# Halves of an array swapped by DMA alone: whole rows on both queues in place of one half of the columns on each

## The chip, the cores and the metric

The kernel runs on one core of a Trainium2 chip. The metric is the device time of one execution in microseconds (us); lower is better. The core has compute engines, which do nothing here but a few start-up fills, and 16 DMA engines, which move the data. SP (SyncE) and ACT (ScalarE) each issue DMAs into a queue of their own, called q1 and q10 in the profile; both queues are served by the same 16 DMA engines.

## The reference

```
x = np.random.randn(8192, 8192).astype(np.float32)
return np.fft.ifftshift(x)
```

With even sizes this swaps the quadrants: `out[r, c] = x[(r + 4096) % 8192, (c + 4096) % 8192]`. There is no arithmetic. 268.44 MB are read from the device's main memory (HBM) and 268.44 MB are written to it. A row has 32 KB, half a row 16 KB; the right half of each source row becomes the left half of a row of the output, and the left half the right.

## The kernel before

Every DMA goes straight from `x` to `out`, both in HBM. `copy` (lines 28 to 33) issues one: it is given a queue, a first row and column of the output, and the dimensions as pairs of step and count, which hold for both sides; line 29 works out where the source begins. `rows` is 16 x 16 = 256, so the 8192 rows make 32 blocks of 256.

The loops of lines 43 to 48 go through the blocks from the last to the first, four at a time. For each block SP's queue moves the left half of the output rows (line 45: 256 pieces of 16 KB, 4 MB) and ACT's queue a right half (line 48), in the order 1, 0, 3, 2 within the four while SP goes 3, 2, 1, 0. A DMA of 256 rows has 16 neighbouring rows for each DMA engine. Thus SP reads only right halves of `x` and writes only left halves of `out`, and ACT the other way round.

One of ACT's DMAs, that of the block that begins at `start` (line 35), leaves out its last 16 rows (line 47) and has 240. Those 16 half rows are moved ahead of the loops in four strips of 1024 columns (4 KB). Three of the strips are cut into two DMAs, of 14 and 2, 9 and 7, and 4 and 12 rows, and the fourth has all 16 rows (lines 36 to 41): seven DMAs with 64 pieces in all.

The order in a queue is the order of the program. The framework gives the DMAs eight completion semaphores in turn, and an issue waits until the DMA that last used its semaphore has landed; so four of a queue's large DMAs are under way at a time. Nothing else is waited for until the end, where SP waits for the last of them (line 74).

Of the kernel before, what the change touches and what calls it, by code (L numbers as in the profile page):

```python
# [1 line left out]

# [4 lines left out]


ENGINES = 16


@with_exitstack
def kernel(
    ctx: ExitStack,
    tc: tile.TileContext,
    x: bass.AP,
    out: bass.AP,
):


    nc = tc.nc
    R, C = x.shape
    hr = R // 2
    hc = C // 2
    per = 16
    rows = ENGINES * per

    def copy(queue, row, col, dims):
        src = (row + hr) % R * C + (col + hc) % C
        queue.dma_start(  # L30
            out=bass.AP(out.tensor, out.offset + row * C + col, dims),
            in_=bass.AP(x.tensor, x.offset + src, dims),
        )

    start = R - 3 * rows
    strip = hc // 4
    for n, k in enumerate((14, 9, 4)):
        col = hc + n * strip
        copy(nc.scalar, start + rows - ENGINES, col, [[C, k], [1, strip]])
        copy(nc.scalar, start + rows - ENGINES + k, col, [[C, ENGINES - k], [1, strip]])  # L40
    copy(nc.scalar, start + rows - ENGINES, hc + 3 * strip, [[C, ENGINES], [1, strip]])

    for first in range(R - 4 * rows, -1, -4 * rows):
        for n in (3, 2, 1, 0):
            copy(nc.sync, first + n * rows, 0, [[C, rows], [1, hc]])
            right = first + (n + 2) % 4 * rows
            left_out = ENGINES if right == start else 0
            copy(nc.scalar, right, hc, [[C, rows - left_out], [1, hc]])


# [1 line left out]
_INS = ['x']  # L52
_OUTS = [((8192, 8192), 'float32')]


# [23 lines left out]
```

## Time and profile before

| | us |
|---|---|
| median of 3 runs | 822.09 (822.01 to 822.77) |
| profiled execution | 821.95 |
| its span, first to last instruction | 820.2 |
| SP's issues, first to last | 0.7 to 700.4 |
| ACT's issues, first to last | 0.7 to 726.2 |
| from issue to landing, a 4 MB DMA (median) | 101.7 (SP), 102.0 (ACT) |

The profile counts what the 16 DMA engines moved as packets; a packet here is one piece of a DMA on one engine, and a completion write of 4 bytes counts as a packet as well. "GB/s" is what was read, and as much was written in the same time. The span is shown in 40 slices of 20.5 us each. A DMA issue is short on the engine that issues it; its landing is the time at which all of its data and its completion have arrived. The line number of all issues is that of the helper, line 30.

### The profile page before, as it was taken

To read this page: it belongs to the slowest core of one execution; us is meant where nothing else is said; L and a number is where in the kernel's file an instruction comes from. 1 tells how busy PE (TensorE), PEld (TensorE's weight loads), DVE (VectorE), ACT (ScalarE), POOL (GpSimd) and SP (SyncE) were. 2 spreads that over 40 slices of the span, in tenths; PEclk is the share of its full clock that TensorE was granted. 3 is DMA by queue.
4 is the path that set the end of the run, shared out by engine and by line. 5 is a ranking of instruction groups with operands and counts; after the bars stand their busy time and mean duration, and the time that the engine had idled before them with its cause. 6 is when DMAs were issued, how large, how long until landed. Compare 5 with 4: busy or idle time off the path is not lost. (4 is left out here: it accounts for less than half of the span.)

```text
span 820.2 us, 116 instructions
## 1 busy us (share of the span) xinstructions
POOL 0.2 (0%) x4
## 2 busy tenths in 40 slices
POOL 0000000000000000000000000000000000000000
DMA  9999999999999999999999999999999999999998
GB/s 301 329 324 331 331 328 326 327 330 333 335 330 327 332 328 329 332 329 333 324 331 328 322 336 328 332 324 329 328 328 331 327 333 329 328 330 331 325 328 285
DMA packets 17520, 268.44 MB, mean 327 GB/s; under 512 B 1088, under 2 KB 1088, under 8 KB 1152
## 3 DMA queue, kind: packets, MB, share of 16 engines
q1 hardware_dynamic: 8704, 134.22, 51.3%
q10 hardware_dynamic: 8816, 134.22, 47.9%
HBM read 268.44 MB, written 268.44 MB: 655 GB/s over the span
## 5 line engine op out<-in xcount | busy, mean ns | idle before, releaser
L63 POOL MEMSET const-uint8-127<- 128x1 uint8 x1 | 0.1, 103 | 0.0
L63 POOL MEMSET const-bfloat16-1.0<- 128x1 bf16 x1 | 0.1, 102 | 0.0
L63 POOL MEMSET const-float32-0.0<- 128x1 f32 x1 | 0.1, 99 | 0.2 <-issue 0.2
L63 POOL MEMSET const-float32-1.0<- 128x1 f32 x1 | 0.1, 99 | 0.0
## 6 DMA issues: line engine op xcount, KB each, us to landing
out_dram<-in_x_dram SPq DMA_DIRECT2D x32, 4096.0 KB, 101.7
out_dram<-in_x_dram ACTq DMA_DIRECT2D x31, 4096.0 KB, 102.0
out_dram<-in_x_dram ACTq DMA_DIRECT2D x1, 3840.0 KB, 29.3
out_dram<-in_x_dram ACTq DMA_DIRECT2D x1, 64.0 KB
out_dram<-in_x_dram ACTq DMA_DIRECT2D x1, 56.0 KB
out_dram<-in_x_dram ACTq DMA_DIRECT2D x1, 48.0 KB
out_dram<-in_x_dram ACTq DMA_DIRECT2D x1, 36.0 KB
out_dram<-in_x_dram ACTq DMA_DIRECT2D x1, 28.0 KB
```

The lines of the kernel that those rows point to most:

```text
L63: nc = _bacc.Bacc("TRN2", target_bir_lowering=False, num_devices=1)
```

## The change

`copy`, the strips and the two-column loop are replaced by `whole_rows`, which issues one DMA for both halves of 256 rows (512 pieces of 16 KB, 8 MB). The dimensions have one more pair: within a row, two halves. On one side the second half lies `hc` elements after the first, on the other `hc` before it, since the halves swap; the step there is negative and the start is at `hc`. Both queues are called with `right_first` False, so that each row's left half of the output (from the right half of the source) comes first and its right half second.

The loop goes through the 32 blocks from the first to the last, four at a time: SP moves blocks 0 and 1 of the four, ACT blocks 2 and 3. Each queue has 16 DMAs of 8 MB, all of one size. A DMA engine still has 16 neighbouring rows of each block, now with both halves.

```
-    per = 16
-    rows = ENGINES * per
+    rows = ENGINES * 16
+    blocks = R // rows
 
-    def copy(queue, row, col, dims):
-        src = (row + hr) % R * C + (col + hc) % C
+    def whole_rows(queue, block, right_first):
+        row = block * rows
+        src = (row + hr) % R
+        to = [[C, rows], [hc, 2], [1, hc]]
+        back = [[C, rows], [-hc, 2], [1, hc]]
+        if right_first:
+            dst, dims, of = hc, back, 0
+            dims_of = to
+        else:
+            dst, dims, of = 0, to, hc
+            dims_of = back
         queue.dma_start(
-            out=bass.AP(out.tensor, out.offset + row * C + col, dims),
-            in_=bass.AP(x.tensor, x.offset + src, dims),
+            out=bass.AP(out.tensor, out.offset + row * C + dst, dims),
+            in_=bass.AP(x.tensor, x.offset + src * C + of, dims_of),
         )
 
-    start = R - 3 * rows
-    strip = hc // 4
-    for n, k in enumerate((14, 9, 4)):
-        col = hc + n * strip
-        copy(nc.scalar, start + rows - ENGINES, col, [[C, k], [1, strip]])
-        copy(nc.scalar, start + rows - ENGINES + k, col, [[C, ENGINES - k], [1, strip]])
-    copy(nc.scalar, start + rows - ENGINES, hc + 3 * strip, [[C, ENGINES], [1, strip]])
-
-    for first in range(R - 4 * rows, -1, -4 * rows):
-        for n in (3, 2, 1, 0):
-            copy(nc.sync, first + n * rows, 0, [[C, rows], [1, hc]])
-            right = first + (n + 2) % 4 * rows
-            left_out = ENGINES if right == start else 0
-            copy(nc.scalar, right, hc, [[C, rows - left_out], [1, hc]])
+    for n in range(0, blocks, 4):
+        for a, b in ((0, 2), (1, 3)):
+            whole_rows(nc.sync, n + a, False)
+            whole_rows(nc.scalar, n + b, False)
```

## The prediction

> **What bounds the kernel now.** I read the page's busy shares and queue rows first, then the issues and their waits, then busy time by stretches of the span, which is the view that the sum is made from.
>
> ```profile
> DMA  9999999999999999999999999999999999999998
> GB/s 301 329 324 331 331 328 326 327 330 333 335 330 327 332 328 329 332 329 333 324 331 328 322 336 328 332 324 329 328 328 331 327 333 329 328 330 331 325 328 285
> DMA packets 17520, 268.44 MB, mean 327 GB/s; under 512 B 1088, under 2 KB 1088, under 8 KB 1152
> q1 hardware_dynamic: 8704, 134.22, 51.3%
> q10 hardware_dynamic: 8816, 134.22, 47.9%
> HBM read 268.44 MB, written 268.44 MB: 655 GB/s over the span
> ```
>
> No compute engine works. The 16 DMA engines are busy in every slice, and the shares of the two queues add up to 99.2% of 16 engines' span. So the time is bytes over rate, with a start and an end around it. Most packets are 16 KB (one half row each). In the trace's packet records the fastest of them take 611 ns; the mean, 0.992 x 820.2 us x 16 engines over some 16,400 packets, is 0.79 us. The engines are thus not idle but slowed, in something that they share.
>
> ```profile
> SPq L30 <- DMA out_dram<-in_x_dram: 683.0, 29, 25.6
> SPq L74 <- DMA out_dram<-in_x_dram: 118.3, 3, 101.8
> ...
> L30 ACTq DMA_DIRECT2D out_dram<-in_x_dram x39: 518/518/1389, 0.7 to 726.2; - x39
> L30 SPq DMA_DIRECT2D out_dram<-in_x_dram x32: 511/511/607, 0.7 to 700.4; - x32
> ```
>
> The first two are SP's own waits, the others the issues by engine: an issue takes 0.5 us, and SP waits at line 30 because four of its DMAs are already under way (25.6 us a wait, 102 us from issue to landing). The queues never run dry, so issuing costs nothing. SP's last issue, at 700.4, lands some 102 us later, near 802; ACT's last, at 726.2, lands at 819.4. So ACT works alone over the last 17 us, and in the packet records ACT moves no 16 KB packet before 22 us, only 64 packets of 4 KB.
>
> ```profile
> 0.00:2.00 2.00, 0.20 (x4) 1.00 0.00 0
> ...
> 4.00:5.00 1.00, 0.00 (x0) 1.00 1.00 426
> ...
> 8.00:16.00 8.00, 0.00 (x0) 1.00 1.00 325
> 16.00:22.00 6.00, 0.00 (x0) 1.00 0.99 324
> ...
> 42.00:782.00 740.00, 0.00 (x0) 1.00 1.00 329
> 782.00:802.00 20.00, 0.00 (x0) 1.00 1.00 333
> 803.00:815.00 12.00, 0.00 (x0) 1.00 0.99 322
> ...
> 817.00:818.00 1.00, 0.00 (x0) 1.00 0.48 180
> 818.00:820.20 2.20, 0.00 (x0) 1.00 0.04 15
> ```
>
> The columns are the stretch, its length, POOL, clock, DMA share, GB/s. Nothing moves for 2 us; both queues together give 329 GB/s; one queue alone gives 325, 324 and 322, weighted over 26 us (8 x 325 + 6 x 324 + 12 x 322) / 26 = 323.4. The end falls off within some 3 us. At 329 GB/s the whole copy is 268.44 MB / 0.329 = 815.9 us, and each GB/s more or less is 2.5 us. The sum below stands against the profiled execution's 821.95 us (span 820.2 and 1.75 around it), which is 0.14 under the median of 822.09.
>
> **The change part by part.**
>
> *Both queues from start to end.* The strips of lines 35 to 41, which keep ACT's large DMAs back, go, and both queues have 16 equal DMAs. ACT should start within a microsecond or two of SP and end as close behind it. The 26 us of one queue then run at 329 instead of 323.4: 26 x 5.6 / 329 = -0.4 us. Bounds: 0 (stretches of 10 to 15 us with both queues also vary, 320 to 339, so the gap may be chance) and -0.6 (all 26 us at the last one's 322). I take -0.4.
>
> *Fewer completions.* Packets under 512 B are the completion writes, 1088 now: 64 large DMAs x 16 engines + 64 of the strips. After: 32 DMAs x 16 = 512. 576 fewer at 9 ns (packet records) over 16 engines: -0.3 us. Nothing hides it, as the engines are always busy.
>
> *Strips as packets.* 64 packets of 4 KB at a mean of 224 ns, over 16 engines, 0.90 us, become 16 of 16 KB at 0.79 us: -0.1 us.
>
> *The ramp between engines.* The strips go to the first 14, 2, 9, 7, 4, 12 and 16 engines, if a DMA of k rows uses the first k: seven 4 KB pieces on the first engine and one on the last, 24 KB apart, 1.5 packets or 1.2 us. Without them all engines have equal bytes. If the ramp evens out a real difference, the last engine ends half of it later, +0.6; if it does not, half of it earlier, -0.6. The last DMA's 16 completions lie from 817.0 to 819.4 with the ramp in, wider than the ramp itself, so it hardly does harm: I take +0.6.
>
> *Issues.* 32 of 8 MB in place of 71. An issue of 256 half rows takes 0.51 to 0.61 us; one of 512 I bound between that and twice it. Behind it lie three DMAs of that queue, 4 x 51 = 204 us from issue to landing, so it costs nothing; without that cover it would be 32 x 0.5 us shared over two issuers, 8 us. Only the first is uncovered: data begin at 2.15 us now, and a longer list before the first packet could add 0 to 0.6. I take 0, since each engine needs only its first entry to begin.
>
> *The distance of the queues.* In the change the queues are always two blocks (16 MB) apart. Now SP is ahead by more than a block, and by the DMAs' landings the blocks that the two write together lie 0, 1, 3 or 4 apart. I asked for every such stretch and weighted them: 328.3, 329.4, 329.3 and 329.5 GB/s. That distance is worth nothing that can be seen: 0.
>
> *The order of the halves.* This is the term that decides. Now one queue always reads right halves and writes left ones, the other the reverse, so that an engine taking packets from both in turn changes halves at every packet; with one queue it never does. In the change both queues begin with the left half: SP left, ACT left, SP right, ACT right. If the engine takes turns, the half changes at every second packet. No row shows that; it lies between 329 (always) and 323.4 (never). If the whole gap, 830.1 - 815.9 = 14.2 us, came from the halves, half of the handovers would cost 7.1 us; if it comes from having one queue or from chance, 0. A gain from touching 32 KB of one row in two packets that follow each other on a queue isn't excluded: the best long stretch with both queues, 333 GB/s, bounds it at -9.8. Both one- and two-queue rows are equally near; I take the middle of 0 and 7.1, +3.5.
>
> Sum: -0.4 - 0.3 - 0.1 + 0.6 + 3.5 = +3.3, or **825.3 us**.
>
> A rule speaks against the first and last of these terms: the Trainium skill, "DMA: Bandwidth & Descriptors", Rules for kernel authors, says that spreading DMAs over several issuing engines doesn't raise bandwidth, since all run on the same 16 engines and only issue time is saved. By that rule the 322 to 325 is chance, both terms are 0, and the sum would be +0.2. Here 26 us at 323.4 against 740 us at 329 lean the other way, but stretches of that length have shown 320 too.
>
> **Rivals.**
>
> *The rate is held* (no change). For it: the distance of the blocks changes nothing, and 40 slices stay within 322 to 336. Against it: one queue alone was slow three times out of three. The sum without its last term: 821.95 - 0.2 = 821.8 us.
>
> *Whole rows go faster.* For it: packets reach 611 ns whenever the rest lets them, and 426 GB/s was seen for a microsecond; an engine would stay on one 32 KB row for two packets of a queue. Against it: now, too, a queue's next packet is only 32 KB away, and nothing made it go over 333 for long. At 333: 806.1 in place of 815.9, so -9.8 - 0.2, 812.0 us.
>
> *The two queues move in step* (the slower side). Both start together with equal DMAs, so each engine holds the same row and half of two blocks 16 MB apart, and all 16 engines, with no strips to stagger them, sit at the same place 512 KB apart. They then act as one queue does: 323.4 throughout, 14.2 - 0.2 = +14.0, 836.0 us. It decides from the first microseconds, and only if the engines stay within about a packet of each other. Against it: now ACT's engines finish a 25.5 us DMA within 1 us of each other early on and 3.5 us at the end, so step is lost. The Trainium skill, "DMA: Bandwidth & Descriptors", Latency and other measured facts, reports copies of 16 KiB rows at about half rate where the row pitch is 4 or 8 MiB, and suspects lock-stepped streams; that 0, 1, 3 and 4 blocks of 8 MB give the same rate here speaks against it in this trace.
>
> *The change doesn't do what it says*: the backward step in the source makes the rows come in smaller pieces. By the 4 KB packets (224 ns, four of them 0.90 against 0.79 us), +13% of 815.9, some 926 us. The half row stays contiguous on both sides, which speaks against it.
>
> **How the numbers follow.** Slower through the halves, 823.7 to 829: 0.34. Held, 820.4 to 823.7: 0.20. Faster: 0.28. In step: 0.14. Smaller pieces: 0.04. A measurement of this kernel tells about 0.2% (1.6 us) from no change, by its runs from 822.01 to 822.77. So faster 0.28, within 0.2% 0.20, slower 0.34 + 0.14 + 0.04 = 0.52. The range of 811 to 839 leaves out the best of the faster case (above 333 GB/s, 0.06), the worst of in step (below 322, 0.05) and the smaller pieces (0.04). The likeliest case's own range is 823.7 to 829.
>
> **What would show it.** Packets should fall to 16,896 with 512 small ones, both queues at 8448, and both sides' last issues should land within a few microseconds of each other. The steps hold if slices read 326 to 329 and the last slice no lower than 280. Slices of 329 to 331 mean held, 332 and over means that rows help, 325 and under that the queues are in step. More packets than 16,896 mean that the rows were cut. The prediction is wrong if the rate goes above 329, or if the time grows outside the rate: over 2 us more at the start, or an end longer than some 4 us.

## The result: 5.5% slower, nearly all of it in the rate

The changed kernel takes 868.2 us (median of 4 runs, 866.78 to 868.85), the kernel before 822.43 us beside it: a ratio of 1.0551, 95% interval 1.0531 to 1.057. The profiled execution took 868.85 us, with a span of 867.1.

These lines of the page of the changed kernel answer to those shown of before:

```profile
GB/s 280 313 314 305 313 318 312 309 314 309 311 310 315 311 308 305 320 311 313 310 312 316 311 308 313 306 313 310 311 311 314 311 311 317 311 308 309 305 311 273
DMA packets 16896, 268.44 MB, mean 310 GB/s; under 512 B 512, under 2 KB 512, under 8 KB 512
q10 hardware_dynamic: 8448, 134.22, 49.8%
q1 hardware_dynamic: 8448, 134.22, 49.6%
out_dram<-in_x_dram SPq DMA_DIRECT2D x16, 8192.0 KB, 215.4
```

The DMA engines are as busy as before (49.8 + 49.6 = 99.4%), and the rows were not cut: the packets are the 16,896 that equal halves of rows give. But every slice is slower. The next view is busy time by stretches, with the DMA share and GB/s in the last two columns:

```profile
0.00:2.00 2.00, 0.20 (x4) 1.00 0.00 0
2.00:8.00 6.00, 0.00 (x0) 1.00 1.02 333
8.00:22.00 14.00, 0.00 (x0) 1.00 1.01 300
...
42.00:782.00 740.00, 0.00 (x0) 1.00 1.00 312
```

Over the same 740 us it reads 312 GB/s where the kernel before had 329. 268.44 MB / 0.312 = 860.4 us against 815.9: 44.5 of the 46.9 us by which the spans differ. The start is no later (the first large packet begins at 2.2 us, 2.1 before), and the loss is there from the first DMA on: 300 GB/s from 8 to 22 us, where one queue alone had 324 and 325 before. So the question is what slows the same packets of 16 KB, whose mean goes from 794 to 842 ns in the packet records.

One thing caught the eye at once, in the issues (minimum, median and maximum ns of an issue, then first and last start):

```profile
L39 SPq DMA_DIRECT2D out_dram<-in_x_dram x16: 565/43758/50858, 0.7 to 648.3; - x16
L39 ACTq DMA_DIRECT2D out_dram<-in_x_dram x16: 572/44590/51277, 0.7 to 652.7; - x16
```

Half of the issues take some 44 us or more, not 0.5: the first three of a queue are short, and from the fourth DMA of 512 pieces on most wait, as if the queue were full (that reason is inferred). It looks like the cause of the loss, and it isn't.

### The profile page after: what moved, and what is told of

It reads as the page before. It is cut to its first block, busy times and chain, and to the rows that moved or that the text cites. A ratio compares the mean times of both kernels' runs of the same rounds, so it can differ in the third digit from the quotient of the medians.

```text
span 867.1 us, 77 instructions
## 1 busy us (share of the span) xinstructions
POOL 0.2 (0%) x4
## 2 busy tenths in 40 slices
DMA packets 16896, 268.44 MB, mean 310 GB/s; under 512 B 512, under 2 KB 512, under 8 KB 512
## 3 DMA queue, kind: packets, MB, share of 16 engines
q10 hardware_dynamic: 8448, 134.22, 49.8%
q1 hardware_dynamic: 8448, 134.22, 49.6%
HBM read 268.44 MB, written 268.44 MB: 619 GB/s over the span
```

## Experiments

The runs were made on several chips. The kernel before took 811 us on the three chips of the first three batches and 820 to 822 us on the others, so each run is told as a ratio to the kernel before on its own chip. Runs f to i, but for i3, issue the DMAs from a plain program with four completion semaphores for each queue, where nothing else is said.

**First batch: which part of the change costs.**

*e1: ACT turned round.*

```
-            whole_rows(nc.scalar, n + b, False)
+            whole_rows(nc.scalar, n + b, True)
```

> Only ACT's order is turned round: it moves the right half of each output row first, so that SP and ACT are on opposite halves at every turn, as in the kernel before. Theory A (the two queues being on the same half at the same turn costs the 17 GB/s): the rate returns to about 329 GB/s and the time to 821 to 826 us. Theory B (both queues in step at 16 MB, without strips), theory C (DMAs of 512 pieces fill the queue: the fourth issue takes 46 us) and theory D (a queue that flips halves inside a row is slow by itself): it stays at 310 to 313 GB/s, 865 to 870 us.

Measured: 1.0374 (1.0344 to 1.0404), 320 GB/s. The time alone is inconclusive: here the two queues also drifted apart, SP's last issue being at 537 us and ACT's at 756, so more than the order of the halves changed. But they drifted only after some 215 us. From 22 to 215 us, with the halves turned round and the queues 5 us apart, e1 read 319 GB/s; f1 below, with the halves as in the changed kernel and on a chip on which the kernel before takes the same 811 us, read 319 over the same stretch. So theory A falls already here.

*e2: half rows, without strips, ascending, in step.*

```
+    for first in range(0, blocks, 4):
+        for n in (0, 1, 2, 3):
+            half_rows(nc.sync, first + n, False)
+            half_rows(nc.scalar, first + (n + 2) % 4, True)
```

> DMAs of 256 half rows as in the kernel before (SP all left halves, ACT all right halves), but without strips, from the first block to the last and with the queues two blocks apart and in step. Theory B (in step at 16 MB and no stagger, or the ascending order): about 865 us with 311 GB/s. Theories A, C and D: as the kernel before, 820 to 824 us.

Measured: 1.0029 (1.001 to 1.0047). Taking the strips away, going upwards, and two blocks between the queues cost 0.3% together.

*e3: the changed kernel's blocks, left halves first, then right halves.*

```
+            for right in (False, True):
+                half_rows(nc.sync, n + a, right)
+                half_rows(nc.scalar, n + b, right)
```

> The blocks and the order of the queues as in the changed kernel, each DMA cut into two of 256 pieces: all 256 left halves, then all 256 right halves, both queues on the same half. Theory A (same half on both queues at a turn): 860 us or more, since the halves never mix within a DMA. Theory B: about 865 us. Theory C (full queue) and theory D (flipping within a row): 820 to 826 us.

Measured: 1.0058 (1.0031 to 1.0086). Both queues are on the same half for four fifths of the time (ACT is 5 us of 25 behind), and it costs 0.6%, at most 0.9%.

*e4: 128 whole rows a DMA.*

```
-    rows = ENGINES * 16
+    rows = ENGINES * 8
```

with the blocks regrouped so that the queues stay 512 rows apart.

> Whole rows in the same order of halves, with 128 rows a DMA (256 pieces, 4 MB), so that four DMAs fit in a queue as before; an engine has 8 neighbouring rows and the queues stay 16 MB apart. Theory C (full queue): back to 820 to 826 us and issues of 0.5 us. Theories A, B and D: 862 to 872 us with short issues.

Measured: 1.001 (0.9999 to 1.0022). Its page and its issues:

```profile
GB/s 305 329 337 335 330 332 329 329 338 335 333 329 335 336 325 337 335 328 333 334 330 333 335 328 334 334 335 331 334 334 337 336 333 331 335 332 331 333 334 301
```

```profile
L39 ACTq DMA_DIRECT2D out_dram<-in_x_dram x32: 570/570/887, 0.7 to 711.0; - x32
L39 SPq DMA_DIRECT2D out_dram<-in_x_dram x32: 562/562/659, 0.7 to 706.2; - x32
```

The whole loss is gone, with the same halves in the same order on both queues. Two explanations remained: the issues are short again, so the full queue (theory C); or something in DMAs of 256 rows.

**Second batch: the full queue.** Number of rows a DMA, and how many DMAs a queue may have under way.

*f1: 256 rows, 4 under way.* 

> The changed kernel's 32 DMAs in the same order, with the kernel's own semaphores, four DMAs under way on a queue: a control. Every theory: slower than the kernel before by 4.5 to 6%, issues of 40 us and more once the queue is full.

Measured: 1.0439 (1.034 to 1.0537). The control repeats the loss. That it is 4.4% here and 5.3 to 5.5% on the slower chips (i3 and the result) is not explained.

*f2: 256 rows, 2 under way* (`DEPTH = 2`). 

> As the control, but only two DMAs under way on a queue (2 x 33 pieces and completions on an engine instead of 4 x 33). Theory C (a full queue slows the transfers): within 1% of the kernel before, issues of under 1 us. Theory P (16 whole rows for each engine, 512 KB apart, collide in memory) and theory S (a DMA of 512 pieces is slow by its shape): as the control, 4.5 to 6% slower.

Measured: 1.0436 (1.0344 to 1.0528).

*f3: 128 rows, 8 under way* (`ROWS = 128`, `DEPTH = 8`). 

> 128 whole rows a DMA, as in the run that was as fast as the kernel before, but eight under way on a queue (8 x 17). Theory C: 4 to 6% slower than the kernel before, issues of 20 us and more. Theories P and S: within 1%.

Measured: 0.9997 (0.9976 to 1.0017).

*f4: half rows, 8 under way.* 

> Half rows, SP left and ACT right, in step, 256 pieces a DMA, eight under way on a queue. Theory C: 4 to 6% slower than the kernel before although no row is moved whole, issues of 20 us and more. Theories P and S: within 1%, as with four under way.

Measured: 1.0004 (0.9974 to 1.0034). The issues of f2, then those of f3:

```profile
L32 SPq DMA_DIRECT2D out_dram<-in_x_dram x16: 564/565/660, 0.7 to 737.5; - x16
```

```profile
L32 SPq DMA_DIRECT2D out_dram<-in_x_dram x32: 602/23534/58496, 0.7 to 648.1; - x32
```

Theory C falls on both sides. f2 has short issues and is as slow as f1; f3 waits 23 us or more in half of its issues and loses nothing. A long issue costs nothing while the queue behind it is full.

**Third batch: size or addresses.** An engine has a DMA's rows in one piece: with 256 rows, 16 rows or 512 KB, and the engines' pieces lie 512 KB apart. With 128 rows it is 256 KB, with 512 rows 1 MB. (The packet records name no engine and no address; that an engine's rows are neighbours is borne out below by the beat, two in a DMA with 16 rows an engine and four in one with 32.) Larger DMAs have more pieces too, so the next runs part the two.

*g1: every second row.* 

> Whole rows, but each DMA of 256 rows cut into two of 128: its even rows, then its odd rows (256 pieces, 4 MB each). The 16 engines stay 512 KB apart as in the changed kernel and each keeps its 16 rows. Theory P (engines that move whole rows 512 KB apart collide in memory): 3 to 6% slower than the kernel before. Theory S (a DMA of some 500 pieces is slow by its size): within 1%.

```
+                whole(sync, n + a + odd, 128, 2)
+                whole(scalar, n + 512 + a + odd, 128, 2)
```

Measured: 1.0005 (0.9989 to 1.0021).

*g3: 512 rows.* 

> 512 whole rows a DMA (1024 pieces; 32 rows an engine, the engines 1 MB apart, the queues one DMA apart, 16 MB). Theory P: as slow as the changed kernel or slower, 4 to 12%. Theory S: slower still than the changed kernel, since the DMA is twice as large. If it is within 1%, both fall and 512 KB is special.

Measured: 1.2696 (1.2534 to 1.2857), 1028 us, the largest effect of all. Its busy time by stretches, over one DMA of SP (each engine sweeps 32 rows in 129 us, 256 KB in 32 us; the cuts are at every 256 KB):

```profile
256.40:261.60 5.20, 0.00 (x0) 1.00 0.99 299
261.60:288.70 27.10, 0.00 (x0) 1.00 0.98 248
288.70:293.90 5.20, 0.00 (x0) 1.00 0.97 309
293.90:321.00 27.10, 0.00 (x0) 1.00 1.00 255
321.00:326.20 5.20, 0.00 (x0) 1.00 0.99 290
326.20:353.20 27.00, 0.00 (x0) 1.00 1.01 257
353.20:358.40 5.20, 0.00 (x0) 1.00 1.02 328
358.40:385.50 27.10, 0.00 (x0) 1.00 1.00 245
```

Note the beat: 290 to 328 GB/s for the 5 us after each 256 KB, 245 to 257 for the rest. 5 us is ACT's lag behind SP (5.0 to 5.6 us by the completions in this run): for so long SP's engines have passed into the next 256 KB and ACT's have not. A DMA of 1024 pieces has no reason to beat every quarter of itself; an address does. Averaged over all DMAs by row of the sweep, from the packet records, the same beat is in the changed kernel (GB/s; the first figure is the engine's first row; 16 rows are 512 KB):

```
after, by SP's rows   324 324 304 308 304 307 305 312   326 323 307 308 308 309 303 309
g4, by SP's rows      317 315 334 331 331 331 334 330   320 312 327 330 333 332 330 334
h3, by SP's rows      322 326 330 326 328 323 328 327   324 328 326 325 327 327 329 325
i1, one queue         330 312 311 312 314 310 308 316   329 314 310 318 312 310 310 317
```

*g4: ACT half a block off.*

```
+    whole(scalar, R - 256, 128)
...
+    whole(scalar, R - 128, 128)
```

> 256 whole rows a DMA as in the changed kernel, but ACT begins and ends with a DMA of 128 rows, so that its engines are half a block (8 rows, 256 KB) behind or ahead of SP's in their 16 rows. In the changed kernel the rate was 319 to 330 GB/s in the first two and the ninth and tenth of an engine's 16 rows, where one queue has passed a 256 KB boundary and the other has not, and 303 to 312 elsewhere. Theory Q (engines on the same 256 KB half of their 512 KB are what collides): within 1% of the kernel before. Theory P without Q, and theory S: 3 to 6% slower.

Measured: 1.0185 (1.0152 to 1.0217), between the theories. ACT completes each DMA 19 us before SP, which is 5.9 of 16 rows, so the queues are on different 256 KB for six rows in eight and on the same for two. The table shows 327 to 334 in the six and 312 to 320 in the two: the line of the changed kernel turned over, with the same DMAs.

The same can be read in the other runs with two queues. Sort each half microsecond of the packet records by whether the two queues, by their completions, stand in the same 256 KB of the engines' 512 KB (1 MB in g3) or not: 309 and 324 GB/s in the changed kernel, 316 and 331 in f1, 253 and 310 in g3, 316 and 332 in g4. It also settles e1, where the rates are 317 and 330: its drifting queues shared the 256 KB for 70% of the time instead of 82%, and f1's two rates mixed by 70 to 30 give the 320 GB/s that e1 had. Half rows and every second row show no loss by it (335 and 331 in e2, 333 and 334 in g1).

**Fourth batch: the addresses by themselves.**

*h1: 240 rows.* 

> 240 whole rows a DMA (480 pieces; an engine has 15 neighbouring rows, the engines are 480 KB apart, the queues 15 MB), with one DMA of 128 rows at the end of each half of the array. Theory Q (all engines and both queues on the same 256 KB half of 512 KB): no common half is left, within 1% of the kernel before. Theory S (a DMA of some 500 pieces is slow by its size): 3.5 to 6% slower.

Measured: 1.0316 (1.0286 to 1.0346). A miss for theory Q: no common 256 KB, and still 3.2%. (An earlier layout of 240 rows, g2, would have read past the end of `x` in one DMA and has no time; h1 begins anew at the middle of the array.)

*h2: 496 rows.* 

> 496 whole rows a DMA (992 pieces; 31 rows an engine, the engines 992 KB apart), against the 1024 pieces and 1 MB that cost 27%. Theory Q, addresses: within 2% of the kernel before. Theory S, size: 20 to 27% slower.

Measured: 1.0098 (1.0069 to 1.0128). With 992 pieces a DMA costs 1%, with 1024 it cost 27%. The size of the DMA is out.

*h3: ACT six rows off.* 

> The changed kernel's DMAs of 256 whole rows, with ACT beginning with one of 96 rows and ending with one of 160, so that with its own lag of 1.5 rows it is 7.5 of an engine's 16 rows away from SP, nearly half of the 512 KB (it was 6.5 on the other side in the run with 128 rows, which was 1.85% slower and still slow for two rows in eight). Theory Q: the queues are on different 256 KB halves nearly all the time, within 1% of the kernel before. Theory S: 3.5 to 6% slower.

Measured: 1.0101 (1.0072 to 1.013). The completions lie 25.6 us of 51.4 apart, just half, and the beat is gone: 322 to 330 in every row. What the changed kernel loses is down to a fifth, by nothing but a shift between the queues.

*h4: every second row of 512.*

```
+            whole(sync, n + odd, 256, 2)
+            whole(scalar, n + 512 + odd, 256, 2)
```

> DMAs of 256 whole rows that are every second row of 512 (even, then odd): 512 pieces as in the changed kernel, the engines 1 MB apart as in the run that cost 27%, an engine's rows 64 KB apart. Theory P (the distance of the engines alone): 20 to 27% slower. Theory S (512 pieces): 3.5 to 6% slower. Theory D (what costs is that all engines dwell in one 256 KB for long; every second row halves that): within 2%, as every second row of 256 was.

Measured: 1.0008 (0.9992 to 1.0024). From its page:

```profile
GB/s 298 330 328 328 329 325 327 335 329 322 337 318 330 330 333 330 336 325 327 331 326 324 335 325 328 332 331 326 332 332 330 327 329 332 330 329 330 329 327 298
DMA packets 16896, 268.44 MB, mean 327 GB/s; under 512 B 512, under 2 KB 512, under 8 KB 512
```

The same number of DMAs and packets as in the changed kernel, with engines 1 MB apart as in g3, and no loss. So the distance of the engines alone (theory P) does not do it either: it takes neighbouring rows.

**Fifth batch: engines among themselves or queues?**

*i1: one queue, 256 rows.* 

> The same DMAs of 256 whole rows, all 32 on SP's queue, block after block. Theory E (the 16 engines, 512 KB apart, collide among themselves): as slow as the changed kernel, 4 to 7% slower than the kernel before, and no faster rows after a 256 KB boundary. Theory Q2 (it takes two queues on the same 256 KB half): as fast as one queue with 128 rows, within 3% of the kernel before.

*i2: one queue, 128 rows.* 

> The control for it: 64 DMAs of 128 whole rows, all on SP's queue (an engine has 8 rows, the engines 256 KB apart). Both theories: within 3% of the kernel before; what it costs is the price of having one queue, which the prediction put at up to 1.7%.

*i3: the changed kernel again.* 

> The changed kernel as it stands, on the same chip as the two runs with one queue, since the chips differ (the kernel before took 811 us on one and 822 on another): 4 to 6% slower than the kernel before.

Measured: 1.0439 (1.0408 to 1.0471), 1.0015 (1.0003 to 1.0027) and 1.0532 (1.0509 to 1.0555). The pages of i1 and then i2:

```profile
GB/s 292 310 320 312 317 315 318 311 317 314 321 310 310 317 317 314 312 314 313 312 319 313 316 312 316 317 310 307 310 310 317 322 313 312 320 317 313 311 319 288
```

```profile
GB/s 298 327 329 329 331 325 328 325 329 325 331 329 331 323 331 322 330 331 329 331 325 327 329 329 330 325 325 326 329 329 333 326 325 326 329 329 325 329 331 304
```

With one queue the loss is there without any second one: the 16 engines do it among themselves. Theory E's side note fell: there are faster rows in i1 as well, one after each 256 KB (330 and 329 in the table), while the engines, whose completions spread over 1.0 to 1.7 us against 1.67 us a row, pass the boundary one by one. The second queue matters by where it is: mostly in the same 256 KB the loss is 5.3% (i3), half an engine's share away 1.0% (h3). One sweep of 256 KB takes 13 us in i1 and 12.6 us in g1, so theory D (how long the engines dwell in one 256 KB) falls too.

**What is shown, and what stays open.** Shown: the loss belongs to sweeps over neighbouring whole rows; it is 4.4 to 5.5% where the engines' starts lie 512 KB apart and 27% at 1 MB, and it vanishes at 256 KB (e4, f3, i2). In these runs the distance is also the length of an engine's sweep; the length by itself isn't it, since 31 neighbouring rows at 992 KB cost 1% (h2). The loss is smaller while the two queues stand in different 256 KB (h3, g4, and the sorting above). It needs neither a full queue, nor two queues, nor a DMA of a certain size, nor an order of halves. That memory serves all these streams from the same part, chosen by address bits from 256 KB up, would fit the beat and the shifts, but it is inferred. Open is why sweeps that leave gaps, every second row and half rows, escape at the same distances (g1, h4, e2, e3), and why engines 480 KB apart (h1) still lose 3.2% where 992 KB apart (h2) lose 1%: some loss needs no power of two.

## Why the prediction was wrong

It said slower by 3.3 us through the order of the halves, 825.3 us in a range of 811 to 839. It is slower by 46 us, for another reason. By its own steps:

- *Both queues from start to end, -0.4.* The step rests on one queue alone being slower (323.4 against 329 over 26 us). It isn't in i2, which runs the whole copy on one queue at 1.0015, about 1.2 us, and reads 328 GB/s from 42 to 782 us. The text named chance as the other reading; that is the likely one, though no run has half rows on one queue throughout. The Trainium skill's rule that spreading DMAs over issuing engines brings no bandwidth ("DMA: Bandwidth & Descriptors", Rules for kernel authors) agrees with i2 against e4 (1.0015 and 1.001).
- *Completions and strips, -0.4.* The packets fell to 16,896 and 512 as worked out; 0.4 us can't be told apart beside 46.
- *The ramp between engines, +0.6.* The end got no worse: the last DMA's completions lie 1.3 us apart in the changed kernel (865.0 to 866.3) and 2.4 us apart before. e2, without the ramp, bounds all of its price with the order of the blocks at 0.8 to 3.8 us (0.1 to 0.47% of 811).
- *Issues, nothing.* The length was far off (bounded at about 1 us, measured 44), and the answer right: f2 and f3 show that it costs nothing behind a queue that is full.
- *The distance of the queues, nothing.* Right for half rows, where it was measured, and wrong to carry over: with whole rows, moving one queue by half of an engine's 16 rows is worth some 4% (h3 at 1.0101 against i3 at 1.0532).
- *The order of the halves, +3.5, the term that decided.* This is the step that failed, in its cause and in its size. It kept the rate between 329 and 323.4 GB/s; the rate was 312. e4 has just this order on both queues and costs 0.1%, e3 keeps both queues on the same half most of the time and costs 0.6%, and e1 turns the order and keeps the loss while the queues are in step. The lower bound, 323.4, was the mean of the one-queue rows in the trace of before, taken for the slowest rate that there could be. No row showed 16 engines sweeping neighbouring whole rows 512 KB apart, and by the runs that is what took the 44.5 us.

The rival *in step* came nearest: "all 16 engines, with no strips to stagger them, sit at the same place 512 KB apart". Its price, 836 us, again came from the one-queue row, and it was given 0.14 for two reasons that the runs undo. That distances of 0, 1, 3 and 4 blocks gave the same rate was an observation on half rows, which lose little at these distances (0.3% in e2, 0.6% in e3). That the engines fall out of step doesn't hold here: over the whole run the completions of a DMA spread over 1.2 to 2.3 us, no more at the end than at the start, where the kernel before went from 1 to 3.5.

The Trainium skill's row on HBM pitch at large powers of two ("DMA: Bandwidth & Descriptors", Latency and other measured facts), set beside that rival, was the warning to heed. It gives 207 of 214 GB/s at 512 KiB and about half rate at 4 and 8 MiB, and it suspects streams in lock step; it speaks of the pitch of rows. Here, with the distance between the engines' shares in its place, it was 312 of 329 at 512 KB (95%) and 1.27 times the time at 1 MB. The runs agree with its direction and differ in the condition: at the same 512 KB and 1 MB, every second row lost nothing.

Of the signs that the text named, slices of 325 and under, which point to "in step", came: all but the first and last read 305 to 320, and the last, 273, is under the 280 named. Its signs for being wrong outright, a rate above 329 or time lost outside the rate, did not come. Two readings in the working are off and move nothing: the fastest packet of 16 KB takes 608 ns, not 611, and the slices that stay within 322 to 336 are 38 of the 40.

## What to carry to other kernels

When a copy changes what each DMA engine walks through, write down where all 16 engines stand at one moment and how far apart; here 512 KB or 1 MB cost 4 to 27% where the engines swept neighbouring whole rows, and halving the rows of a DMA (256 to 128) took the whole loss away. The slowest row of a trace bounds only what that trace did: for an access pattern that it doesn't hold, the bound on the slow side is open. And fold the rate over one DMA's period before believing the first oddity: the 44 us issues were the striking thing in the profile and worth nothing, while the beat at 256 KB led to the cause.

## What the runs showed of the hardware that had not been expected

- The first three DMAs of 512 pieces of a queue were issued in under 1 us each, the fourth took 47 and 51 us, and the median was 44; with 256 pieces and four under way all went through in some 0.5 us, and with eight allowed the median issue took 23.5 us. The transfers did not suffer.
- ACT's queue stayed some 5 us behind SP's (4.1 to 5.6 by the median of a DMA's completions) from the first DMA to the last but one, in every run but e1 where both had equal DMAs and started together. In e1 ACT began 5 us ahead and the queues drifted up to 166 us apart; why is open.
- One queue moves the array as fast as two in DMAs of 128 whole rows (1.0015), and no version here was measurably faster than the kernel before: the ratios of e4, f3, f4, g1 and h4 lie between 0.9997 and 1.001.
